# Seven block products in place of eight for the first product of an MLP, with sums of weight blocks formed by accumulating DMAs

## The chip, the cores and the metric

The kernel runs on one NeuronCore of a Trainium2 chip. The metric is device time in microseconds (us). Engines are called by the profile's names: PE is TensorE's matmul stream and PEld its weight loads, DVE is VectorE, ACT ScalarE, POOL GpSimd, SP SyncE.

## The reference

Two decoder layers on 512 tokens of 1024 channels, in fp32. Each layer runs a mixer (the first: gated MLP and latent attention; the second: gated linear attention) with an output projection, and then an MLP of inner width 4096:

```python
def sqrelu_mlp(x, w1, w2):
    return jnp.square(jax.nn.relu(x @ w1)) @ w2
...
        x = layer_norm(ALPHA * x + y, ln1_g[layer], ln1_b[layer])
        x = layer_norm(ALPHA * x + sqrelu_mlp(x, w_ff1[layer], w_ff2[layer]), ln2_g[layer], ln2_b[layer])
```

## The kernel before

**Products.** Every fp32 operand is held as a pair, hi (rounded to fp32r) and lo (the rest). A product is three matmuls, hi x hi, hi x lo and lo x hi, added up in one PSUM bank (`mm3`, L158 to L161). A weight granule of 128x1024 (512 KB, `granule`, L129) is loaded on SP's queue, cast by ScalarE to hi (L137) and reduced by VectorE to lo (L138). `to_xT` (L188) transposes a token block of the residual XN by TensorE into PSUM and splits it into XH and XL (`split`, ScalarE L164 and VectorE L165). XH and XL hold x transposed, 8 blocks of 128 channels by 512 tokens.

**The MLP.** `ff` (L276) works in four parts of the inner width. The first product of a block of 128 inner channels (`ff1_block`, L291) is 24 matmuls of 512 columns (tokens); `relu2` (L281) makes the squared relu and its pair hh, hl. The second product (`ff2_half`, L308) takes 8 inner blocks for each token block and half of the model's columns, 24 matmuls of 512 columns, and VectorE adds the result to XN (`add_cols`, L208).

**The opening.** The output projection's steps come from the generator `norms` (L243): the LayerNorm of token block t is under the products of block t+1, and its transposes stand after six of eight channel blocks of that block's second half. The norm of the last block has no products of its own behind it, so `open_blocks` (L334) computes the first four inner blocks on the first 256 tokens, 24 matmuls of 256 columns each; after three of them it transposes block 3.

**The closing.** The last part's second product is issued block by block: in the first layer through `norms` again (`close_blocks`, L362), in the second with the final norm and the stores (`close_final`, L350, `ln_store`, L225).

**What sets the order.** TensorE and VectorE run in the order in which the program writes their instructions (`manual_schedule`; for VectorE through `in_order`, L266, around the MLPs). Each engine is a queue: an instruction that waits holds all behind it. The other engines' order is the framework's. PSUM has eight banks of 128x512: six in a cycle for products, two for transposes (`BANKS`, L122).

Of the kernel before, what the change touches and what calls it, by code (L numbers as in the profile page):

```python
# [12 lines left out]
F32 = mybir.dt.float32  # L13
F32R = mybir.dt.float32r
# [89 lines left out]
def trunk(ctx: ExitStack, tc: tile.TileContext, a: dict, out: bass.AP):  # L104
# [24 lines left out]
    def granule(src, kb, cols, pool=wp, raw=None):  # L129
        """hi, lo of kb blocks of P rows by cols columns of a weight matrix."""  # L130
# [11 lines left out]
    def weave(a, b, n):  # L142
        """n pieces of a after each piece of b, until both are done."""
# [23 lines left out]
    def rsqrt_(var, n, eps=LN_EPS):  # L167
        """1/sqrt(var + eps) for a [P, n] fp32 tile, by Newton's iteration."""
# [19 lines left out]
    def to_xT(src, k0, nk, t):  # L188
        """XH/XL[:, k0:k0+nk, block t] <- the transposes of nk [P, P] blocks of src."""
# [15 lines left out]
    def add_cols(t, cols, acc, first, stats=()):  # L205
        """XN[:, t, cols] <- XN (alpha * XN at first) + acc; stats: where its statistics go, part by part."""
# [9 lines left out]
    def ln_block(t, stats):  # L216
        """XN[:, t] <- LN(XN[:, t])."""
# [7 lines left out]
    def ln_store(t, stats):  # L225
        """out[block t] <- LN(XN[:, t]); the root is ScalarE's, corrected by a step of Newton's iteration."""
# [16 lines left out]
    def norms(mm, stats):  # L243
        """The products mm(t, n, k0, k1) of half n of token block t, each block's norm under the next block's products.

        A generator: yields after each half."""
        for t in range(NT):
# [3 lines left out]
            if t > 0:  # L251
                block_T(t - 1)
# [7 lines left out]
    def act_stat(acc, lh, ll, g, per, ks, last):  # L260
        """acc += (lh + ll)[:, k, :]^T w over the blocks ks; g are granules of per blocks."""
# [11 lines left out]
    def ff1_granules(layer, f, pool=wp):  # L273
        return granules(a["w_ff1"][layer], 0, D, 4, slice(f * P, (f + 2) * P), pool)

    def ff(layer, hp, fp, xp, out_proj, prefetch):  # L276
        """The layer's MLP, after the rest of out_proj's steps; returns what prefetch returned."""
        w2 = a["w_ff2"][layer]
        hs, gr = {}, {}

        def relu2(f, acc, cols):  # L281
            hh, hl = hs[f]
            n = cols.stop - cols.start
            r = fp.tile([P, S], F32, tag="r", name="r")
            q = fp.tile([P, S], F32, tag="q", name="q")
            nc.scalar.activation(r[:, :n], acc[:, :n], AF.Relu)  # L286
            nc.scalar.activation(hh[:, cols], r[:, :n], AF.Square)  # L287
            nc.vector.tensor_tensor(q[:, :n], r[:, :n], r[:, :n], ALU.mult)  # L288
            nc.vector.tensor_tensor(hl[:, cols], q[:, :n], hh[:, cols].bitcast(F32), ALU.subtract)  # L289

        def ff1_block(f, cols=slice(0, S)):  # L291
            if f not in hs:
                hs[f] = (hp.tile([P, S], F32R, tag="hh", name="hh"), hp.tile([P, S], F32R, tag="hl", name="hl"))
            g = gr[f // 2 * 2]
            acc = bank("f1")
            n = cols.stop - cols.start
            jc = slice(f % 2 * P, (f % 2 + 1) * P)
            for k in range(KD):
                wh, wl = g[k // 4]
# [824 lines left out]
```

## Time and profile before

| what | value |
|---|---|
| median of 3 runs (lowest to highest) | 1193.89 us (1192.4 to 1194.69) |
| span of the profiled execution | 1190.5 us |
| profiled execution's own time | not given apart from its span; the runs lie 1.9 to 4.2 us above it |
| PE busy | 1174.2 us, 5880 matmul instructions |
| DVE busy | 669.3 us |
| ACT busy | 420.2 us |
| POOL busy | 4.6 us |
| moved by DMA | 111.53 MB |

The span is the time from the first to the last instruction that the profiler recorded. Busy times are sums over the instructions of an engine. The matmuls' own durations overlap, since they are pipelined; the price of one is therefore read from the distance of two starts.

### The profile page before, as it was taken

The numbers are of one execution on the slowest core, as the hardware profiler recorded it, in microseconds if no ns is written. First come the engines' busy times: TensorE is split into PE (matmuls) and PEld (weight loads), VectorE is DVE, ScalarE is ACT, GpSimd is POOL, SyncE is SP. The second block draws the span as 40 slices with busy tenths as digits, with TensorE's granted clock in tenths as the row PEclk, the third lists the DMA queues.
The fourth block names the chain that finished last, engine by engine and source line by source line (L and its number), as shares of the span: only waits on it lengthen the run. The fifth ranks groups of instructions, "written<-read, shape, count | busy, mean of one in ns | idle before, by whom it ended". The sixth has DMA issues, their size and how long they took to land.

```text
span 1190.5 us, 14854 instructions
## 1 busy us (share of the span) xinstructions
PE 1174.2 (99%) x5880; PEld 968.9 (81%) x5880; DVE 669.3 (56%) x1392; ACT 420.2 (35%) x663; POOL 4.6 (0%) x13
## 2 busy tenths in 40 slices
PE   8999999999999999999999999999999999999997
PEld 8988788988888888888888888778888888888886
DVE  6745698745245244267758569998451451451546
ACT  5466452342142133152264333332331241241410
POOL 0000000000000000000000000000000000000000
PEclk9999999999999999999999999999999999999999
DMA  8413142224134134152225312212251251251411
GB/s 251 135 36 124 44 136 63 75 93 141 36 106 141 36 107 141 36 189 72 57 92 142 106 37 71 71 53 72 75 172 36 73 174 37 72 166 46 141 36 54
DMA packets 84197, 111.53 MB, mean 94 GB/s; under 512 B 6080, under 2 KB 53056, under 8 KB 84128
## 3 DMA queue, kind: packets, MB, share of 16 engines
q1 hardware_dynamic: 84128, 110.59, 29.6%
q8 instruction: 46, 0.75, 0.3%
q14 instruction: 23, 0.19, 0.0%
HBM read 108.47 MB, written 2.10 MB: 93 GB/s over the span
## 4 chain that ended last, share of the span: by engine, by line
PE 95%; DVE 2%; ACT 1%; DMA 0%; issue 0%; SPq 0%; DVEq 0%; ACTq 0%
PE f L159 20%; PE f L161 20%; PE f L160 20%; PE vg L159 3%; PE vg L160 3%; PE vg L161 3%; PE op L159 2%; PE op L161 2%; PE op L160 2%; PE sc L607 1%; PE xt L194 1%; PE qk L159 1%; PE qk L160 1%; PE qk L161 1%; PE o L629 1%; PE pl L888 1%
## 5 line engine op out<-in xcount | busy, mean ns | idle before, releaser
L137 ACT CAST whi<-raw 128x1024 fp32r<-128x1024 f32 (+3 forms) x189 | 194.0, 1029 | 344.3 <-DMA raw<-in_w_ff 177.2
L138 DVE TENSOR_TENSOR wlo<-raw,whi 128x1024 fp32r<-128x1024 f32 (+3 forms) x189 | 220.8, 1196 | 55.7 <-ACT whi L137 55.3
L161 PE MATMUL f<-XH,wlo 128*128 128x512 f32 (+1 forms) x576 | 213.4, 370 | 0.0
L159 PE MATMUL f<-XH,whi 128*128 128x512 f32 (+1 forms) x576 | 213.3, 370 | 0.0
L160 PE MATMUL f<-XL,whi 128*128 128x512 f32 (+1 forms) x576 | 213.3, 370 | 0.0
L159 PE MATMUL f<-whi,hh 128*128 128x512 f32 (+1 forms) x520 | 203.5, 391 | 0.0
L160 PE MATMUL f<-wlo,hh 128*128 128x512 f32 (+1 forms) x520 | 203.3, 391 | 0.0
L161 PE MATMUL f<-whi,hl 128*128 128x512 f32 (+1 forms) x520 | 203.3, 391 | 0.0
L208 DVE SCALAR_TENSOR_TENSOR XN<-XN,f 128x512 f32<-128x512 f32 (+1 forms) x65 | 44.1, 678 | 191.3 <-PE f L161 191.3
L159 PEld LDWEIGHTS f<-XH,whi 128*128 128x128 f32 x576 | 108.4, 188 | 20.5
L160 PEld LDWEIGHTS f<-XL,whi 128*128 128x128 f32 x576 | 108.2, 188 | 20.3
L161 PEld LDWEIGHTS f<-XH,wlo 128*128 128x128 f32 x576 | 108.2, 188 | 20.3
L288 DVE TENSOR_TENSOR q<-r 128x512 f32<-128x512 f32 (+1 forms) x72 | 45.4, 631 | 140.0 <-ACT r L286 140.0
L160 PEld LDWEIGHTS f<-wlo,hh 128*128 128x128 f32 x520 | 97.7, 188 | 22.6
L161 PEld LDWEIGHTS f<-whi,hl 128*128 128x128 f32 x520 | 97.7, 188 | 22.6
L159 PEld LDWEIGHTS f<-whi,hh 128*128 128x128 f32 x520 | 97.7, 188 | 22.6
L286 ACT ACTIVATE r<-f 128x512 f32<-128x512 f32 (+1 forms) x72 | 39.5, 548 | 143.8 <-PE f L161 143.8
L164 ACT CAST XH<-xt 128x512 fp32r<-128x512 f32 x44 | 24.2, 588 | 91.0 <-PE xt L194 90.7
L159 PE MATMUL vg<-whi,XH 128*128 128x512 f32 x128 | 53.0, 414 | 0.0
L159 PE MATMUL op<-whi,XH 128*128 128x512 f32 x128 | 52.1, 407 | 0.2 <-ACT XH L164 0.2
L289 DVE TENSOR_TENSOR hl<-q,hh 128x512 fp32r<-128x512 f32 (+1 forms) x72 | 45.6, 633 | 9.5 <-ACT hh L287 2.6
L161 PE MATMUL op<-whi,XL 128*128 128x512 f32 x128 | 50.7, 396 | 0.0
(222 smaller groups left out, 1540.9 us busy)
## 6 DMA issues: line engine op xcount, KB each, us to landing
raw<-in_w_ff SPq DMA_DIRECT2D x128, 512.0 KB, 4.2
raw<-in_w_in_odd SPq DMA_DIRECT2D x24, 512.0 KB, 4.0
XN<-in_x SPq DMA_DIRECT2D x16, 256.0 KB, 2.9
raw<-in_w_in_even SPq DMA_DIRECT2D x8, 512.0 KB, 3.9
raw<-in_w_out_even SPq DMA_DIRECT2D x8, 512.0 KB, 3.7
raw<-in_w_out_odd SPq DMA_DIRECT2D x8, 512.0 KB, 3.4
LB<-in_ln_b SPq DMA_DIRECT2D x4, 512.0 KB, 3.8
LG<-in_ln_g SPq DMA_DIRECT2D x4, 512.0 KB, 3.8
```

Source lines behind the costliest of these rows:

```text
L137: nc.scalar.copy(hi[:, :n], raw[:, :n])
L138: nc.vector.tensor_tensor(lo[:, :n], raw[:, :n], hi[:, :n].bitcast(F32), ALU.subtract)
L159: nc.tensor.matmul(acc, lh, rh, start=first, stop=False)
L160: nc.tensor.matmul(acc, lh, rl, start=False, stop=False)
L161: nc.tensor.matmul(acc, ll, rh, start=False, stop=last)
L164: nc.scalar.copy(hi, src)
L194: nc.tensor.transpose(pt[:, j * P:(j + 1) * P], src[:, (k + j) * P:(k + j + 1) * P], ident)
L208: nc.vector.scalar_tensor_tensor(x, x, ALPHA if first else 1.0, acc, ALU.mult, ALU.add)
L286: nc.scalar.activation(r[:, :n], acc[:, :n], AF.Relu)
L288: nc.vector.tensor_tensor(q[:, :n], r[:, :n], r[:, :n], ALU.mult)
L289: nc.vector.tensor_tensor(hl[:, cols], q[:, :n], hh[:, cols].bitcast(F32), ALU.subtract)
L607: nc.tensor.matmul(sc[:, :N], qts[t][:B_QK, h, :], KT[:, h, :N], start=True, stop=True)
```

## The change

Strassen's scheme, in Winograd's form, splits the first product x W1 into 2x2 blocks: the tokens into two halves of 256, the 1024 channels into two of 512, and the inner width into two of 2048. Seven products of blocks take the place of eight. Four of them need a sum of blocks of x (s1 to s4), four a sum of blocks of the weights (t1 to t4), and the results are put together from them:

- P1 = A11 B11, P2 = A12 B21, p3 = s4 B22, p4 = A22 t4, p5 = s1 t1, p6 = s2 t2, p7 = s3 t3 (A blocks of x, B blocks of the weights).
- The work goes in 8 groups of 256 columns of each half of the inner width. `product` issues one of the seven for a group: 24 matmuls of 256 columns into the two halves of a bank. P1 and P2 add up in one bank (C11). V is p6 with P1, X is V with p5; C22, C12 and C21 are differences of X or V and the banks of p7, p3 and p4. p4 goes into the bank that p7 had. V and X lie in LG and LB, the LayerNorm's tiles; its gains are loaded after the last group.
- `terms1` makes the weights' sums. A block's raw fp32 granule is split into hi and lo, and then, in place, two accumulating DMAs of GpSimd's queue (256 KB each) add the next block of weights from HBM to it; when both have landed, the sum is split in its turn. B11 becomes t1, t2 and t4 in this way, one after the other, and B22 becomes t3. B21 is only loaded.
- `x_T` replaces `block_T` in the output projection's steps: for blocks 0 and 1 it also copies the transposes, and for blocks 2 and 3 it forms the sums of the blocks two apart: four operations and five splits on VectorE.
- The second product takes 4 inner blocks at a time (12 matmuls of 512 columns), group by group, and the closing does so with the last group.
- `wseq` is the order of the splits, `slots` that of the products; `upto` issues splits ahead of a slot, up to `TERMS`, and loads up to `LOADS` further ahead.

```diff
+    HALF_S, HK_, GF = S // 2, KD // 2, 2 * P
+    PRODUCTS = {"P1": ("A11", "B11"), "P2": ("A12", "B21"), "p3": ("s4", "B22"), "p4": ("A22", "t4"),
+                "p5": ("s1", "t1"), "p6": ("s2", "t2"), "p7": ("s3", "t3")}
+    ff_T = {}
...
-                mm3(acc[:, :n], wh[:, k % 4, jc], wl[:, k % 4, jc], XH[:, k, cols], XL[:, k, cols], k == 0, k == KD - 1)
-            relu2(f, acc, cols)
...
-        def ff2_half(p, n):
-            for t in range(NT):
-                acc = bank("f2")
-                ff2_mm(p, t, acc, gr[p, n], 0, 8)
-                add_half(t, n, acc, p == 0, None)
...
-            for f in range(4):
-                ff1_block(f, slice(0, 256))
-                if f == 2:
-                    block_T(NT - 1)
-                    items[1][0]()
-            for f in range(4):
-                ff1_block(f, slice(256, 512))
...
+        def x_T(t):
+            v = lambda z: z.rearrange("p (k c) -> p k c", k=HK_)
+            pts = []
+            for h in range(2):
+                pt = bank("xt", "tp")
+                for j in range(HK_):
+                    nc.tensor.transpose(pt[:, tb(j)], XN[:, t, (h * HK_ + j) * P:(h * HK_ + j + 1) * P], ident)
+                pts.append(pt)
+            if t < 2:
+                for h, pt in enumerate(pts):
+                    xr[t, h] = fp.tile([P, S], F32, tag="q", name="xr")
+                    nc.scalar.copy(xr[t, h], pt)
+                    operand(("A11", "A12")[h], t, v(pt))
+                return
+            s1, s2 = (fp.tile([P, S], F32, tag="q", name="sx") for _ in range(2))
+            s3, s4 = xr[t - 2, 0], xr[t - 2, 1]
+            nc.vector.tensor_tensor(s3, s3, pts[0], ALU.subtract)
+            nc.scalar.copy(s1, pts[1])
+            nc.vector.tensor_tensor(s1, s1, pts[0], ALU.subtract)
+            nc.vector.tensor_tensor(s2, s3, pts[1], ALU.add)
+            operand("s1", t, v(s1))
+            operand("s3", t, v(s3))
+            nc.vector.tensor_tensor(s4, s2, s4, ALU.subtract)
+            operand("s2", t, v(s2))
+            operand("s4", t, v(s4))
+            operand("A22", t, v(pts[1]))
...
+        w1v = lambda i, j, g: w1[i * 512:(i + 1) * 512, j * 2048 + g * GF:j * 2048 + (g + 1) * GF].rearrange(
+            "(k p) c -> p k c", p=P)
+        chains, got_w = {}, {}
+        SOURCE = {"B11": (0, 0), "B22": (1, 1), "B21": (1, 0)}
+        NEXT = {"B11": ("t1", (0, 1)), "t1": ("t2", (1, 1)), "t2": ("t4", (1, 0)), "B22": ("t3", (0, 1))}
+
+        def load1(g, n):
+            if n in SOURCE:
+                raw = chains[g, n] = xp.tile([P, WG], F32, tag="cr", name="cr", bufs=4)
+                nc.sync.dma_start(raw.rearrange("p (k c) -> p k c", k=HK_), w1v(*SOURCE[n], g))
...
+                split(hi, lo, raw)
...
+            got_w[g, n] = his, los
+            if n in NEXT:
+                to, src = NEXT[n]
+                for k in range(0, HK_, 2):
+                    nc.gpsimd.dma_start(raw.rearrange("p (k c) -> p k c", k=HK_)[:, k:k + 2], w1v(*src, g)[:, k:k + 2],
+                                        accum_op=ALU.add)
+                chains[g, to] = raw
...
+        def product(g, n):
+
+            first = (g, RELEASED[n]) not in banks
+            if first:
+                banks[g, RELEASED[n]] = bank("f1")
+            acc = banks[g, RELEASED[n]]
+            op, w = PRODUCTS[n]
+            xh, xl = ops[op]
+            his, los = got_w.pop((g, w))
+            for j in range(2):
+                d = acc[:, j * HALF_S:(j + 1) * HALF_S]
+                for k in range(HK_):
+                    for i, (l, r) in enumerate(((his[j][:, k], xh[:, k]), (his[j][:, k], xl[:, k]), (los[j][:, k], xh[:, k]))):
+                        nc.tensor.matmul(d, l, r, start=first and j == k == i == 0, stop=j == 1 and k == HK_ - 1 and i == 2,
+                                         skip_group_check=True)
...
+            V = LG[:, g % 2 * 512:(g % 2 + 1) * 512]
+            X = LB[:, g % 2 * 512:(g % 2 + 1) * 512]
...
+            def c22():
+                r = fp.tile([P, S], F32, tag="q", name="c22")
+                nc.vector.tensor_tensor(r, X, bk("d"), ALU.subtract)
+                relu2(g, 1, 1, r, r)
...
+            def c21():
+                nc.vector.tensor_tensor(bk("d"), bk("d"), V, ALU.subtract)
+                relu2(g, 1, 0, bk("d"))
+
+            step("p1s", {"P1"}, lambda: nc.scalar.copy(V, bk("a")))
+            step("V", {"p1s", "p6"}, lambda: nc.vector.tensor_tensor(V, bk("b"), V, ALU.subtract))
+            step("X", {"V", "p5"}, lambda: nc.vector.tensor_tensor(X, V, bk("e"), ALU.subtract))
+            step("C11", {"P2"}, lambda: relu2(g, 0, 0, bk("a")))
+            step("C22", {"X", "p7"}, c22)
+            step("C12", {"X", "p3"}, c12)
+            step("C21", {"V", "C22", "p4"}, c21)
...
+        def ff2_half(c, n, t):
+            acc = bank("f2")
+            ff2_mm(c, t, n, acc, 0, 4)
+            add_half(t, n, acc, c == 0, None)
...
+        FIRST = ("P1", "P2", "p5", "p7", "p6", "p3", "p4")
+        LATER = ("P1", "p3", "p5", "p7", "p6", "P2", "p4")
+        slots = [(g, n) for n in FIRST[:2] for g in range(2)] + [(g, n) for g in range(2) for n in FIRST[2:]]
+        wseq = [(g, n) for n in ("B11", "B21") for g in range(2)]
+        wseq += [(g, n) for g in range(2) for n in ("B22", "t1", "t3", "t2", "t4")]
+        for c in range(NG):
+            slots += [("w2", c, n, t) for n in range(2) for t in range(NT)] if c < NG - 1 else []
+            wseq += [("w2", c, n, h) for n in range(2) for h in range(2)]
+            if c + 2 < NG:
+                slots += [(c + 2, n) for n in LATER]
+                wseq += [(c + 2, n) for n in ("B11", "B22", "t1", "t3", "t2", "B21", "t4")]
+        place = {w: i for i, w in enumerate(wseq)}
+        at = {"load": 0, "terms": 0}
+        LOADS, TERMS = 6, 6
...
+        todo = 0
+        for _ in out_proj:
+            todo += 1
+            upto(min(todo, 4), 2)
+        for i, s in enumerate(slots):
+            if s[0] == "w2":
+                need = max(place["w2", s[1], s[2], 1], place["w2", s[1], s[2], 0])
+                upto(min(need + 1 + TERMS, need + 1 + 2 * (s[3] + 1)))
+                ff2_half(s[1], s[2], s[3])
+                continue
+            upto(place[s[0], PRODUCTS[s[1]][1]] + 1 + (TERMS if i > 3 else i))
+            product(*s)
+            if i == 0:
+                x_T(NT - 1)
+        upto(len(wseq))
+        load_ln(a["ln2_g"][layer], a["ln2_b"][layer])
+        got = prefetch() if prefetch else None
+        c = NG - 1
...
-        return norms(mm, stats)
+        return norms(mm, stats, lambda t: ff_T["now"](t))
```

**VectorE at the end of the output projection.** The place is between block 3's first half and its norm. L208 adds a half of the projection to XN, L211 and L220 make statistics, L165 are splits of the transposes of block 2. Before:

```order
L208 SCALAR_TENSOR_TENSOR XN<-XN,op 128x512 [waits PE_49]
L211 BN_STATS st<-XN 128x6 [waits DVE_49]
L165 TENSOR_TENSOR XL<-xt,XH 128x4x128 [waits Activation_49] x2
L208 SCALAR_TENSOR_TENSOR XN<-XN,op 128x512 [waits DMAHW0_49,PE_49]
L211 BN_STATS st<-XN 128x6 [waits DVE_49]
L220 BN_AGGR mv<-st 128x2 [waits DVE_49]
```

and with the change (L319 to L325 are the sums of x blocks, sl and sh their pairs):

```order
L319 TENSOR_TENSOR xr<-xr,xt 128x512 [waits PE_49]
L321 TENSOR_TENSOR sx<-sx,xt 128x512 [waits Activation_49]
L322 TENSOR_TENSOR sx<-xr,xt 128x512 [waits DVE_49,PE_49]
L165 TENSOR_TENSOR XL<-sx,XH 128x4x128 [waits Activation_49]
L165 TENSOR_TENSOR sl<-xr,sh 128x4x128
L325 TENSOR_TENSOR xr<-sx,xr 128x512 [waits DVE_49]
L165 TENSOR_TENSOR sl<-sx,sh 128x4x128 [waits Activation_49]
L165 TENSOR_TENSOR sl<-xr,sh 128x4x128 [waits Activation_49]
L165 TENSOR_TENSOR XL<-xt,XH 128x4x128
L208 SCALAR_TENSOR_TENSOR XN<-XN,op 128x512 [waits PE_49]
L211 BN_STATS st<-XN 128x6 [waits DVE_49]
L220 BN_AGGR mv<-st 128x2 [waits DVE_49]
```

Nine operations for block 2 take the place of two splits, ahead of the last half's addition and the norm of block 3.

**VectorE in the opening of the MLP.** cr is the raw granule of the first product's weights, wlo the lo part; a wait for DMASW is one for accumulating DMAs, one for DMAHW for a plain load. Before, the squared relu's operations and splits of plain granules alternate here:

```order
L289 TENSOR_TENSOR hl<-q,hh 128x256 [waits DVE_49,Activation_49]
L165 TENSOR_TENSOR XL<-xt,XH 128x4x128 [waits Activation_49] x2
L138 TENSOR_TENSOR wlo<-raw,whi 128x1024 [waits DMAHW6_49]
L138 TENSOR_TENSOR wlo<-raw,whi 128x1024 [waits DMAHW7_49]
L288 TENSOR_TENSOR q<-r 128x256 [waits Activation_49]
```

and with the change, from the split of t2 of group 0 (its split of t4 is next; then B22, t1 and t3, t2 and t4 of group 1) to V (L435), X (L436) and the difference for C22 (L423) of group 0:

```order
L165 TENSOR_TENSOR wlo<-cr,whi 128x1024 [waits DMASW7_49,DMASW6_49,Activation_49]
L165 TENSOR_TENSOR wlo<-cr,whi 128x1024 [waits DMASW1_49,DMASW0_49,Activation_49]
L165 TENSOR_TENSOR wlo<-cr,whi 128x1024 [waits DMAHW2_49,Activation_49]
L165 TENSOR_TENSOR wlo<-cr,whi 128x1024 [waits DMASW3_49,DMASW2_49,Activation_49] x2
L165 TENSOR_TENSOR wlo<-cr,whi 128x1024 [waits DMASW4_49,DMASW5_49,PE_49,Activation_49]
L165 TENSOR_TENSOR wlo<-cr,whi 128x1024 [waits DMASW6_49,DMASW7_49,PE_49,Activation_49]
L435 TENSOR_TENSOR LG<-f_2758,LG 128x512 [waits PE_49]
L436 TENSOR_TENSOR LB<-LG,f_2694 128x512 [waits DVE_49]
L423 TENSOR_TENSOR c_2785<-LB,f_2727 128x512 [waits DVE_49]
```

The three operations that put group 0's products together stand behind the splits of group 1's t2 and t4.

**TensorE and GpSimd in the same opening.** TensorE goes from p3 of group 0 (sh, sl hold s4) to p4, into the bank that the difference L423 reads:

```order
L407 MATMUL f_2793<-sl,whi 128x256
L407 MATMUL f_2793<-sh,wlo 128x256
L407 MATMUL f_2727<-XH,whi 128x256 [waits DVE_49,Activation_49]
L407 MATMUL f_2727<-XL,whi 128x256
L407 MATMUL f_2727<-XH,wlo 128x256
```

and GpSimd's queue (two DMAs a sum; the pairs shown make t3 and t2 of group 0 and, two pairs later, one sum of group 1):

```order
L359 DMA cr<-in_w_ff 128x2x256 [waits DMAHW1_49,DMAHW7_49,DVE_49,Activation_49]
L359 DMA cr<-in_w_ff 128x2x256
L359 DMA cr<-in_w_ff 128x2x256 [waits DMASW0_49,DVE_49,Activation_49]
L359 DMA cr<-in_w_ff 128x2x256 [waits DMASW1_49]
L359 DMA cr<-in_w_ff 128x2x256 [waits DMAHW0_49,DMAHW2_49,DMASW2_49,DVE_49]
L359 DMA cr<-in_w_ff 128x2x256 [waits DMASW3_49]
```

p4's first matmul waits for VectorE, and each pair of DMAs for the split that used its granule.

## Rows read from the trace of the kernel before

**Rows 1.** The page, parts 1 and 4: busy time per engine; shares of the chain.
```profile
PE 1174.2 (99%) x5880; PEld 968.9 (81%) x5880; DVE 669.3 (56%) x1392; ACT 420.2 (35%) x663; POOL 4.6 (0%) x13
...
PE 95%; DVE 2%; ACT 1%; DMA 0%; issue 0%; SPq 0%; DVEq 0%; ACTq 0%
```

**Rows 2.** Table by stage: the middle of both MLPs (stretch, length, busy, PEclk, DMA).
```profile
232.00:547.00 315.00, 315.00 (x1411) 256.43 (x1410) 134.07 (x158) 101.25 (x130) 0.00 (x0) 1.00 0.33 104
...
832.00:1140.00 308.00, 308.00 (x1383) 250.77 (x1382) 129.60 (x154) 98.13 (x128) 0.00 (x0) 1.00 0.31 98
```

**Rows 3.** Timeline of TensorE, opening of the first MLP: start us, us, instruction.
```profile
222.51 0.28 PE L159 MATMUL f<-XH,whi 128*128 128x256 f32 x1
...
231.03 0.28 PE L161 MATMUL f<-XH,wlo 128*128 128x256 f32 x1
231.15 1.04 PE L194 MATMUL xt<-ident,XN 128*128 128x128 f32 x8
231.94 0.36 PE L159 MATMUL f<-XH,whi 128*128 128x256 f32 x1
...
246.42 0.39 PE L159 MATMUL f<-XH,whi 128*128 128x512 f32 x1
...
251.55 0.40 PE L160 MATMUL f<-XL,whi 128*128 128x512 f32 x1
```

**Rows 4.** VectorE's groups by line and shape: busy us, mean ns, idle before.
```profile
L138 DVE TENSOR_TENSOR wlo<-raw,whi 128x1024 fp32r<-128x1024 f32 x178 | 211.7, 1219 | 54.6 <-ACT whi L137 54.3
...
L288 DVE TENSOR_TENSOR q<-r 128x512 f32<-128x512 f32 x56 | 38.7, 690 | 123.7 <-ACT r L286 123.7
```

**Rows 5.** ScalarE's groups by line and shape, same columns.
```profile
L137 ACT CAST whi<-raw 128x1024 fp32r<-128x1024 f32 x178 | 186.0, 1048 | 341.2 <-DMA raw<-in_w_ff 177.2 <-PE f L161 111.2 <-DMA raw<-in_w_in_odd 20.5
```

**Rows 6.** Timeline of VectorE, end of the first layer's output projection.
```profile
221.49 1.29 DVE L165 TENSOR_TENSOR XL<-xt,XH 128x512 fp32r<-128x512 f32 x2 [3.47 <-ACT XH L164]
222.71 0.69 DVE L208 SCALAR_TENSOR_TENSOR XN<-XN,op 128x512 f32<-128x512 f32 x1
...
227.50 1.29 DVE L223 SCALAR_TENSOR_TENSOR XN<-XN,ny,LB 128x1024 f32<-128x1024 f32 x1
```

**Rows 7.** The page, part 3: DMA queues and kinds (packets, MB, share).
```profile
q1 hardware_dynamic: 84128, 110.59, 29.6%
q8 instruction: 46, 0.75, 0.3%
```

**Rows 8.** DMA issues: queue, count, KB each, median us to landing.
```profile
raw<-in_w_ff SPq DMA_DIRECT2D x128, 512.0 KB, 4.2
...
XN<-in_x SPq DMA_DIRECT2D x16, 256.0 KB, 2.9
...
LB<-in_c_causal SPq DMA_DIRECT2D x1, 256.0 KB, 6.4
```

**Rows 9.** The weight granules' tile, 250 to 300 us, 512 KB loads.
```profile
DMA to landing us min/median/max: 3.3/4.4/6.1
```

**Rows 10.** Table of the last stretches; the column before DMA's is PEclk.
```profile
1182.00:1184.00 2.00, 0.54 (x5) 0.33 (x3) 1.32 (x5) 0.15 (x1) 0.00 (x0) 1.00 0.00 0
...
1186.00:1188.00 2.00, 0.00 (x0) 0.00 (x0) 1.29 (x2) 0.00 (x0) 0.00 (x0) 0.58 0.26 95
1188.00:1190.50 2.50, 0.00 (x0) 0.00 (x0) 0.00 (x0) 0.00 (x0) 0.00 (x0) 0.50 0.35 134
```

**Rows 11.** Timeline of VectorE, closing of the first layer, block 0.
```profile
548.85 0.69 DVE L208 SCALAR_TENSOR_TENSOR XN<-XN,f 128x512 f32<-128x512 f32 x1 [0.39 <-PE f L161]
...
553.63 1.28 DVE L223 SCALAR_TENSOR_TENSOR XN<-XN,ny,LB 128x1024 f32<-128x1024 f32 x1
...
559.60 1.29 DVE L165 TENSOR_TENSOR XL<-xt,XH 128x512 fp32r<-128x512 f32 x2 [3.36 <-ACT XH L164]
```

**Rows 12.** Timeline of VectorE, closing of the second layer, block 0.
```profile
1149.15 0.69 DVE L208 SCALAR_TENSOR_TENSOR XN<-XN,f 128x512 f32<-128x512 f32 x1 [3.99 <-PE f L161]
...
1153.05 1.41 DVE L240 SCALAR_TENSOR_TENSOR XN<-XN,ls,LB 128x512 f32<-128x512 f32 x2
```

More of the change, by code (lines that the diff above doesn't have):

```diff
@@ L251, in norms @@
             if t > 0:
[L252 removed]
+                (bt or block_T)(t - 1)
             mm(t, 1, 6, KD)
@@ new lines, in ff, with operand @@
+        xr = {}
+        def operand(n, t, src):
+            h, l = (z[:, :, (t % 2) * P:(t % 2 + 1) * P] for z in ops[n])
+            split(h, l, src)
+        def x_T(t):
[24 more added lines that the diff above has]
+            operand("A22", t, v(pts[1]))
@@ new lines, in terms1 @@
+        def terms1(g, n, early):
+            raw = chains.pop((g, n))
+            if early:
+                his = [hp.tile([P, HK_, P], F32R, tag="hh", name="wh") for _ in range(2)]
+                los = [hp.tile([P, HK_, P], F32R, tag="hl", name="wl") for _ in range(2)]
+                for j in range(2):
+                    split(his[j], los[j], raw.rearrange("p (k c) -> p k c", k=HK_)[:, :, tb(j)])
+            else:
+                hi, lo = wp.tile([P, WG], F32R, tag="whi", name="whi"), wp.tile([P, WG], F32R, tag="wlo", name="wlo")
+                split(hi, lo, raw)
+                his, los = ([z.rearrange("p (k c) -> p k c", k=HK_)[:, :, tb(j)] for j in range(2)] for z in (hi, lo))
+            got_w[g, n] = his, los
[5 more added lines that the diff above has]
+                chains[g, to] = raw
@@ new lines, in ff, with relu2 @@
+        hq = {}
+        def relu2(g, i, j, src, into=None):
+            hh = hp.tile([P, 2, HALF_S], F32R, tag="hh", name="hh")
+            hl = hp.tile([P, 2, HALF_S], F32R, tag="hl", name="hl")
+            r = into if into is not None else fp.tile([P, S], F32, tag="q", name="r")
+            f = lambda z: z.rearrange("p j t -> p (j t)")
+            nc.scalar.activation(r, src, AF.Relu)
+            nc.scalar.activation(f(hh), r, AF.Square)
+            nc.vector.tensor_tensor(r, r, r, ALU.mult)
+            nc.vector.tensor_tensor(f(hl), r, f(hh).bitcast(F32), ALU.subtract)
+            hq[g][i, j] = hh, hl
@@ new lines, in ff, with upto @@
+        place = {w: i for i, w in enumerate(wseq)}
+        at = {"load": 0, "terms": 0}
+        LOADS, TERMS = 6, 6
+        def upto(n, loads=None):
+            while at["load"] < min(len(wseq), n + (LOADS if loads is None else loads)):
+                w = wseq[at["load"]]
+                at["load"] += 1
+                (load2(*w[1:]) if w[0] == "w2" else load1(*w))
+            while at["terms"] < min(len(wseq), n):
+                w = wseq[at["terms"]]
+                i = at["terms"]
+                at["terms"] += 1
+                (terms2(*w[1:]) if w[0] == "w2" else terms1(*w, i < 4))
@@ L353, in close_final @@
                 st = sm.tile([P, 4, 6], F32, tag="st", name="st", bufs=8)
[L354 to L359 removed]
+                for cols in (slice(0, 512), slice(512, 768), slice(768, D)) if last else (slice(0, 512), slice(512, D)):
+                    m = cols.stop - cols.start
+                    acc = bank("f2")[:, :m]
+                    i, tc_ = t // 2, slice(t % 2 * P, (t % 2 + 1) * P)
+                    n, o = cols.start // 512, cols.start % 512
+                    for k in range(4):
+                        hh, hl = hq[c][i, k // 2]
+                        wh, wl = got_w["w2", c, n, k // 2]
+                        mm3(acc, hh[:, k % 2, tc_], hl[:, k % 2, tc_], wh[:, k % 2, o:o + m], wl[:, k % 2, o:o + m], k == 0, k == 3)
+                    add_cols(t, cols, acc, False, [st[:, i] for i in range(cols.start // 256, cols.stop // 256)])
                 ln_store(t, st)
@@ L373, in close_blocks @@
                 pass
[L375 to L397 removed]
+        (close_final if layer == DEPTH - 1 else close_blocks)()
         return got
```

130 lines of the change are left out of this document (48 added, 82 removed).

## The prediction

> **What bounds the kernel now.** The page's first and fourth parts come first [rows 1]: TensorE is busy 99% of the span, and 95% of the chain that ended last is its own work. So each microsecond in which TensorE stands still, and each microsecond of its work, is a microsecond of the kernel. The table by stage comes second [rows 2]: through the middle of either MLP TensorE is busy without a gap (315 us of 315, 308 of 308), VectorE for 134 and 130 us, ScalarE for 101 and 98. The reader is to see two things: fewer matmul columns would be gained in full, and VectorE and ScalarE have room as long as nothing makes TensorE wait for them.
>
> TensorE's timeline gives the prices [rows 3]. From 222.51 to 231.03 the 256-column matmuls start 71 steps apart, 0.120 us each; from 246.42 to 251.55 the 512-column ones 22 steps apart, 0.233 us each. Two halves cost 3% more than one whole. Each of these matmuls loads its own weights, so narrow matmuls are not held up by weight loads. Eight transposes cost 0.79 us (231.15 to 231.94).
>
> The profiled span is 1190.5 us; the profiled execution's own time is not given apart, and the three runs lie 1.9 to 4.2 us above the span, their median 3.4 above. I make the sum against the span and add 3.4. A measurement of this kernel can tell about 0.2% (2.4 us) from no change.
>
> **What is saved.** The first product of a layer takes 28 whole blocks of 24 matmuls at 0.233 us and 4 blocks in two halves, 48 matmuls at 0.120: 156.8 + 23.0 = 179.8 us. After it: 8 groups of 7 products of 24 matmuls at 0.120 = 161.3 us. That is -18.5 us a layer, **-37.0 us** in all. The second product keeps its 768 matmuls of 512 columns a layer, in groups of half the depth.
>
> **What is added beside TensorE.** From the third group on, one cycle is seven products (20.2 us) and eight halves of the second product (8 x 12 x 0.233 = 22.4): 42.6 us of TensorE. VectorE has in it 11 splits at 1.22, five combinations of products and eight operations of the squared relu at about 0.69, and eight additions at 0.69 [rows 4]: 28 us. ScalarE has 11 casts at 1.05 [rows 5], a copy and eight relu operations near 0.6: 17 us. Both fit below 42.6, so I cost this work at nothing; its cover is gone only where VectorE stands still for landings (the first rival). The loads on SyncE's queue are 512 KB each as before and six ahead of their use, so I cost them at nothing too. The second LayerNorm's loads now come after the last group's products, but 22.4 us of second products cover their landing.
>
> **Wait A: the last token block.** T is the end of the output projection's matmuls (222.51). Before, VectorE has two splits of block 2's transposes, from 221.49, then block 3's addition and norm, from 222.71 to 228.79: 6.08 us [rows 6]. TensorE covers that with 72 matmuls of 256 columns (8.64 us). Now nine operations for block 2 (four sums, five splits) stand at that place in VectorE's order. They can start about 0.6 earlier, without the cast ahead, and take 9 x 0.69 = 6.2 us: from T-1.6 to T+4.65. The norm of block 3 then ends at T+10.7. In TensorE's order only P1 of group 0 (2.88 us) stands ahead of block 3's transposes: it **waits 7.9 us**. Transposes end at T+11.6, then P1 of group 1, P2 of both: T+20.2.
>
> **Wait B: the chain of accumulating DMAs.** VectorE keeps its order. Behind block 3's nine operations (to T+17.5) come the split of B22 and C11's two operations of group 0 and the split of t1, to T+21.4. Call L the time from the end of a split to the landing of both accumulating DMAs issued on it. t2 of group 0 is cast (1.05) and split (1.22) at T+21.4+L+2.3; t4, L+2.3 later; then B22 and t1 of group 1 (1.2 each); t2 and t4 of group 1, each L+2.3 more; and only behind these stand V, X and the difference for C22 (3 x 0.72) of group 0. The first matmul of p4 of group 0 waits for that difference, since p4 goes into the bank that it reads. So p4 starts at T+21.4+4L+13.75. TensorE's work up to there is eight products and the transposes: 23.8 us. Waits A and B together cost **11.4 + 4L** a layer. The same order stands in the second layer.
>
> L is in no row: before, all data moves on one hardware queue, nothing on a software queue and nothing that accumulates [rows 7]. The nearest rows are plain loads [rows 8, 9]: 256 KB land in 2.9 us (a median), 512 KB in 3.3 at the least and 4.2 in the middle, the slowest 256 KB in 6.4. Two accumulating DMAs of 256 KB, issued one behind the other by one engine, each reading what it adds to, should lie between 3.3 us (as fast as the fastest plain load of both) and 12.8 (twice the slowest 256 KB, in series). I take 5.8, twice the 2.9, nearest to two such transfers in series. That gives 34.6 us a layer.
>
> The Trainium skill, "DMA: Bandwidth & Descriptors", section "Anatomy of one DMA — SWDGE (gpsimd) path", fits a DMA on this path by 2.0 us and the bytes over 436 KB a microsecond; no run here shows it. By that an estimate for 512 KB is 3.2 us, and the sum would come to about 1222.
>
> **The clock.** The granted clock is 1.00 up to 1184 and beyond; TensorE stops at 1182.5, and the clock reads 0.58 from 1186 and 0.50 from 1188 [rows 10]. So a long stand brings it to the lower level (1.2 of 2.4 GHz). Waits A and B hold stands of 8 us and, before p4, 23 us. What a restart costs the trace doesn't show: between nothing and half of a low stretch as long as the one seen, 2.1 us. I take 1.5 for each of two stands a layer: 3.0.
>
> Per layer the opening loses 34.6 + 3.0 = 37.6, **+75.2 us** in all.
>
> **The two closings.** The last group of the second product is half as deep: 5.6 us of TensorE a token block instead of 11.2. In the first layer VectorE needs for each block 6.1 (addition to norm), 1.4 for the other half's addition and statistics and 1.3 for the splits [rows 11]: 8.8 us, which 11.2 + 0.8 covered and 5.6 + 0.8 doesn't. TensorE waits before blocks 0, 1 and 2 are transposed 1.4, 2.2 and 2.9 us: +6.5. In the second layer VectorE's block is 1.4 + 5.25 [rows 12] against 5.6, and 1.1 us a block pile up to the end: +4. Together **+10.5**.
>
> **Sum.** 1190.5 - 37.0 + 75.2 + 10.5 = 1239.2; with 3.4 the time is **1243 us**, 4.1% slower. It moves 8 us with each microsecond of L.
>
> **The rivals.** *VectorE's order as the bound of every group.* From the difference for C22 of one group to that of the next, VectorE's order holds five operations of the squared relu and C12 with ScalarE's part between them (about 6 us), the split of B11 (1.2), three landings with a cast and a split behind each (3 x 2.27), four splits of the second product (4.9) and three combinations (2.1): 21 + 3L. That fits into the 42.6 us cycle up to L = 7.2. Beyond it every microsecond of L costs 3 us in six groups of two layers, 36 us, besides the 8: 1254 at 7.2, 1302 at 8.3, 1320 at 8.7. For it: each landing also needs GpSimd to come to its turn, and accumulating may cost a read and a write. Against it: the rows of plain loads lie below. The Trainium skill, "SBUF — State Buffer", section "Who interferes with whom", says that a VectorE operation with two inputs in SBUF contends with GpSimd's reads, and infers that writing descriptors is not held by it; no row here shows either, and a landing that waited for one split (1.22 us) would bring an estimate of 1252. Chance of L over 7.2: 0.22.
>
> *A short L.* At 3.3 the sum is 1223, at 2.5 it is 1216. Slower all the same: the break-even of the sum is at L below zero. Chance of less than 3.3: 0.05.
>
> *Faster: VectorE doesn't hold p4 behind group 1's splits.* If p4 of group 0 waits only for t4 of its own group, it starts at T+26+2L, and the loss is 2.2 + 2L a layer: at L = 3.3, 17.6 in all, one restart a layer 3.0, closings 10.5 against -37.0, which is 1188. It decides below L = 4.6 or so; at 5.8 it gives 1198. Against it: the order on VectorE is fixed by the program, and there group 1's splits stand ahead. Chance 0.10, with what else I misjudge in the same direction.
>
> *The saving isn't there*, because narrow matmuls run slower than counted: the 0.120 us is measured at full clock, weight loads included; it would leave 1280, inside the range. Chance 0.02.
>
> **How the numbers follow.** The sum with L between 3.3 and 7.2 has 0.61 (1223 to 1254), long L 0.22, short L 0.05, the case of p4 released early 0.10 and the missing saving 0.02. The range goes down to 1216 (L = 2.5) and up to 1320 (L = 8.7); it leaves out the 0.10 and about a third of the long L, 0.17. Of the 0.10 some 0.02 ends within 0.2%, and 0.01 of a still shorter L: faster by over 0.2% 0.08, within 0.03, slower 0.89.
>
> **What would show it.** In the changed profile: TensorE's stand of about 8 us before block 3's transposes, and one of about 23 us before p4 of group 0, with the granted clock at the lower level in them; four landings in series on VectorE between t1 of group 0 and V; the middle groups without gaps; a landing of the accumulating DMAs near 5.8 us. If p4 starts without a stand, or the middle has gaps in each group, the step on VectorE's order or the price of L is wrong.

## The result, and the profile after

The changed kernel takes 1551.04 us (1549.85 to 1553.25, 4 runs) against 1194.02 before: a ratio of 1.300, 95% interval 1.298 to 1.302. I had forecast 1243 and a range to 1320. The direction was right, the size was not: the loss is seven times the forecast one.

The page of the changed kernel, parts 1, 3 and 6 (columns as in [rows 1], [rows 7] and [rows 8]):

```profile
PE 1220.1 (79%) x6828; PEld 1060.3 (68%) x6828; DVE 829.1 (54%) x1604; ACT 480.6 (31%) x743; POOL 161.1 (10%) x141
...
q1 hardware_dynamic: 75680, 102.20, 21.1%
q0 software_dynamic: 34816, 33.56, 15.2%
...
cr<-in_w_ff POOLq DMA_DIRECT2D x128, 256.0 KB, 4.5
```

TensorE is busy 79% instead of 99% [rows 1]. There is a second queue, q0, with 128 DMAs of 256 KB. The median of 4.5 us from issue to landing looks harmless beside the 5.8 us that I had taken for a pair.

The table by stage (opening of the first MLP, the middle of the first, the middle of the second; columns as in [rows 2]):

```profile
222.50:315.00 92.50, 30.75 (x202) 29.20 (x200) 32.33 (x48) 19.56 (x27) 14.61 (x12) 0.66 0.31 54
...
332.00:703.00 371.00, 283.13 (x1584) 252.19 (x1584) 154.73 (x189) 93.53 (x117) 57.21 (x47) 0.87 0.41 88
...
1113.00:1487.00 374.00, 285.67 (x1584) 254.24 (x1584) 154.90 (x190) 93.90 (x118) 57.21 (x47) 0.87 0.41 87
```

The middles, without a gap before [rows 2], now leave TensorE idle for a quarter of the time, at a mean granted clock of 0.87. No other engine is full either: VectorE is busy for 155 us of 371, ScalarE for 94.

TensorE's waits (who released it; us in all, times, longest):

```profile
PE f L407 <- DVE c L423: 133.5, 16, 42.2
PE f L407 <- ACT LG L434: 98.5, 12, 10.0
...
PE xt L309 <- DVE XN L223: 15.5, 2, 7.8
```

The third line is wait A: 7.76 and 7.74 us, forecast 7.9. The first is the wait for C22's difference, 42 us in each opening where I had 23. It occurs 16 times, so in every group, where I had two. The second is in no step of the prediction: 12 times, once in every middle group, P2 waits for ScalarE's copy of P1 (L434), since it adds into the bank that the copy reads. On ScalarE that copy stands behind casts, and the first of these waits for a landing (the group whose C22 difference starts at 454.31):

```profile
442.46 1.04 ACT L164 CAST whi<-cr 128x1024 fp32r<-128x1024 f32 x1 [12.03 <-DMA cr<-in_w_ff]
443.41 1.99 ACT L164 CAST whi<-raw 128x1024 fp32r<-128x1024 f32 x2
445.30 0.58 ACT L434 COPY LG<-f 128x512 f32<-128x512 f32 x1
```

### The profile page after: what moved, and what is told of

Its sections match the earlier page's. It is cut to its first block, busy times and chain, and to the rows that moved or that the text cites. A ratio compares the mean times of both kernels' runs of the same rounds, so it can differ in the third digit from the quotient of the medians.

```text
span 1548.5 us, 17378 instructions
## 1 busy us (share of the span) xinstructions
PE 1220.1 (79%) x6828; PEld 1060.3 (68%) x6828; DVE 829.1 (54%) x1604; ACT 480.6 (31%) x743; POOL 161.1 (10%) x141
## 5 line engine op out<-in xcount | busy, mean ns | idle before, releaser
L407 PE MATMUL f<-XH,whi 128*128 128x256 f32 x448 | 157.9, 352 | 257.1 <-DVE c L423 133.5
L165 DVE TENSOR_TENSOR wlo<-cr,whi 128x1024 fp32r<-128x1024 f32 x104 | 125.7, 1222 | 365.1 <-ACT whi L164 365.1
L164 ACT CAST whi<-cr 128x1024 fp32r<-128x1024 f32 x104 | 106.1, 1045 | 532.4 <-DMA cr<-in_w_ff 529.1
L359 POOL DMA_DIRECT2D cr<-in_w_ff x128 | 155.9, 1218 | 1013.9 <-issue 478.0
L407 PE MATMUL f<-XH,wlo 128*128 128x256 f32 x448 | 151.1, 337 | 1.8 <-DVE wlo L165 1.8
L407 PE MATMUL f<-XL,whi 128*128 128x256 f32 x448 | 151.6, 338 | 0.0
L407 PE MATMUL f<-sh,whi 128*128 128x256 f32 x384 | 111.7, 291 | 19.4 <-ACT whi L164 19.4
L407 PE MATMUL f<-sh,wlo 128*128 128x256 f32 x384 | 111.2, 290 | 1.9 <-DVE wlo L165 1.9
L407 PE MATMUL f<-sl,whi 128*128 128x256 f32 x384 | 110.7, 288 | 0.0
L165 DVE TENSOR_TENSOR wlo<-raw,whi 128x1024 fp32r<-128x1024 f32 x64 | 75.6, 1220 | 42.4 <-ACT whi L164 42.4
L208 DVE SCALAR_TENSOR_TENSOR XN<-XN,f 128x512 f32<-128x512 f32 x129 | 81.8, 676 | 12.9 <-PE f L161 12.8
```

What stands on the lines that cost most here:

```text
L164: nc.scalar.copy(hi, src)
L165: nc.vector.tensor_tensor(lo, src, hi.bitcast(F32), ALU.subtract)
L208: nc.vector.scalar_tensor_tensor(x, x, ALPHA if first else 1.0, acc, ALU.mult, ALU.add)
L359: nc.gpsimd.dma_start(raw.rearrange("p (k c) -> p k c", k=HK_)[:, k:k + 2], w1v(*src, g)[:, k:k + 2], accum_op=ALU.add)
L407: nc.tensor.matmul(d, l, r, start=first and j == k == i == 0, stop=j == 1 and k == HK_ - 1 and i == 2, skip_group_check=True)
```

## The account of 358 us

The spans differ by 1548.5 - 1190.5 = 358.0 us. TensorE's timeline of the changed kernel gives the borders, in the opening of the first MLP:

```profile
233.19 1.94 PE L309 MATMUL xt<-ident,XN 128*128 128x128 f32 x8 [7.76 <-DVE XN L223]
...
314.88 0.55 PE L407 MATMUL f<-XH,whi 128*128 128x256 f32 x1 [42.18 <-DVE c L423]
...
331.99 0.38 PE L407 MATMUL f<-XH,whi 128*128 128x256 f32 x1 [0.48 <-DVE c L423]
```

The last two lines are the first matmuls of p4 of groups 0 and 1. The first P1 matmul is at 222.40, so p4 of group 1 starts 109.6 us later. Its thirteen products and the transposes ahead are 38.2 us of work: 71.4 us lost, and 70.2 in the second layer (1004.88 to 1113.24). From there six groups take 371.5 us to p4 of group 7 (703.51), and 374.3 in the second layer, at 42.6 each instead of 61.9: 116 and 119 lost. The saving stands at 37.0. What is left, 358.0 + 37.0 - 141.6 - 235.0 = 18.4 us, lies in the closings and the rest. The measured losses in the table are counted against 38.2 us for an opening and 42.6 for a middle group.

| step | forecast, us | measured, us |
|---|---|---|
| fewer columns | -37.0 | -37.0 (taken as forecast) |
| two openings, clock included | +75.2 | +141.6 |
| twelve middle groups | 0 | +235.0 |
| closings and the rest | +10.5 | +18.4 |

The timeline of GpSimd in the first opening (start us, us; in brackets the idle time ahead):

```profile
243.49 1.21 POOL L359 DMA_DIRECT2D cr<-in_w_ff  x1 [33.63 <-ACT hh L386]
248.36 1.22 POOL L359 DMA_DIRECT2D cr<-in_w_ff  x1 [3.66 <-issue]
253.12 1.21 POOL L359 DMA_DIRECT2D cr<-in_w_ff  x1 [3.53 <-issue]
258.55 1.22 POOL L359 DMA_DIRECT2D cr<-in_w_ff  x1 [4.22 <-DMA cr<-in_w_ff]
266.09 1.21 POOL L359 DMA_DIRECT2D cr<-in_w_ff  x1 [6.32 <-DVE wlo L165]
270.76 1.22 POOL L359 DMA_DIRECT2D cr<-in_w_ff  x1 [3.46 <-issue]
```

VectorE's timeline, the splits of t1 and t2 (two rows):

```profile
244.85 1.22 DVE L165 TENSOR_TENSOR wlo<-cr,whi 128x1024 fp32r<-128x1024 f32 x1
...
264.45 1.22 DVE L165 TENSOR_TENSOR wlo<-cr,whi 128x1024 fp32r<-128x1024 f32 x1 [7.95 <-ACT whi L164]
```

and ScalarE's, the cast of the sum t2 and that of t4 (with two more of the kind):

```profile
263.38 1.04 ACT L164 CAST whi<-cr 128x1024 fp32r<-128x1024 f32 x1 [9.46 <-DMA cr<-in_w_ff]
275.53 2.94 ACT L164 CAST whi<-cr 128x1024 fp32r<-128x1024 f32 x3 [11.10 <-DMA cr<-in_w_ff]
```

The last pair makes t4 of group 0. Its split of t2 ends at 265.67, the DMAs start at 266.09 and 270.76, and ScalarE can cast at 275.53: **L is 9.9 us**. GpSimd is busy 1.2 us with a DMA, yet starts the next only 4.7 us or more after the one before, as long as that takes to land. In the whole trace none of the 128 starts while another is under way, and most start 0.3 us behind the landing of the one before. "issue" in the brackets says that the profile shows nothing that GpSimd waited for. Where t3's pair stands ahead (243.49 and 248.36), t2's, whose split of t1 ended at 246.07, starts at 253.12 and can be cast at 263.38: 17.3 us.

From the split to the cast, the four landings between t1 of group 0 and V take 17.3, 9.9, 18.1 and 9.9 us, 55.15 together. In place of 4L in the prediction's own chain that gives 55.15 + 13.75 = 68.9 us from the end of t1's split (246.07) to p4 of group 0; measured 68.8. In the second layer it is 68.0 and 68.0.

In the middle, with L = 9.9 and 9.4 for one pair ahead, the rule of the first rival gives a cycle of 21 + 3 x 9.9 + 9.4 = 60 us. Measured: 61.9. The size fits better than the parts: in the group whose difference is at 454.31 the pairs of t1, t3 and t2 run one behind another, and the four pairs take 40.6 us where the rule has 39.1, while ScalarE's copy and P2, which stand between t4's landing and the next difference, are not in the rule. There t4's first DMA took longer to land, and the second started that much later (GpSimd's timeline, then the landing of the first):

```profile
431.15 1.21 POOL L359 DMA_DIRECT2D cr<-in_w_ff  x1 [6.19 <-DVE wlo L165]
437.90 1.21 POOL L359 DMA_DIRECT2D cr<-in_w_ff  x1 [5.54 <-issue]
...
DMA to landing us min/median/max: 6.4/6.4/6.4
```

Why it took longer, no run shows.

## The experiments

Theories: **Q**, the software queue's room for descriptors lets GpSimd issue only one such DMA until it has landed; **G**, GpSimd needs 4.7 us to prepare one; **A**, adding in the DMA engines is slow; and, apart from these, that VectorE's order alone makes the loss. The runs e1 to e6 are single ones; the kernel before took 1192 us (the median) beside them.

**e1_plain.**

```diff
-                    nc.gpsimd.dma_start(raw.rearrange("p (k c) -> p k c", k=HK_)[:, k:k + 2], w1v(*src, g)[:, k:k + 2],
-                                        accum_op=ALU.add)
+                    nc.gpsimd.dma_start(raw.rearrange("p (k c) -> p k c", k=HK_)[:, k:k + 2], w1v(*src, g)[:, k:k + 2])
```

> The change with the same DMAs on GpSimd's queue, but overwriting in place of adding (so the sums of weight blocks are left out). Theory Q (the software queue has room for only one accumulating DMA of 256 rows at a time, so GpSimd holds the next back until the one before has landed: starts 4.7 us apart): a plain DMA needs less of that room, starts come about 1.2 us apart, a pair lands 6 to 7 us after its split, and the time falls to 1350 to 1450 us. Rival G (GpSimd needs 4.7 us to prepare each DMA, adding or not): no change, 1540 to 1560 us. Rival A (adding itself is slow in the DMA engines): as fast as under Q; the next run tells them apart.

Measured: 1268.35 us, below what Q gave. GpSimd's timeline shows a pair from 254.08:

```profile
254.08 1.44 POOL L359 DMA_DIRECT2D cr<-in_w_ff  x2 [5.78 <-DVE wlo L165]
```

Two DMAs, 0.72 us each, without a pause. On the page they land in 3.4 us (the median):

```profile
cr<-in_w_ff POOLq DMA_DIRECT2D x128, 256.0 KB, 3.4
```

G falls for plain DMAs. Q and A are both left.

**e2_quarter.**

```diff
-                for k in range(0, HK_, 2):
-                    nc.gpsimd.dma_start(raw.rearrange("p (k c) -> p k c", k=HK_)[:, k:k + 2], w1v(*src, g)[:, k:k + 2],
+                for k in range(HK_):
+                    nc.gpsimd.dma_start(raw.rearrange("p (k c) -> p k c", k=HK_)[:, k:k + 1], w1v(*src, g)[:, k:k + 1],
```

Each DMA now adds one block of 128 rows, 128 KB.

> The change with each sum made by four accumulating DMAs of 128 KB in place of two of 256 KB. Theory Q: three of these have room at once, starts come 1 to 2 us apart, and four land 6 to 8 us after the split in place of 9.9: 1380 to 1460 us. Rival G by the piece: four starts at 4.7 us, a landing after 19 us, over 1800 us. Rival G by the row, and rival A: the same total, 1520 to 1570 us.

Measured: 1352.8 us, better than Q had it and against G and A, which gave no gain. The same bytes are added in the same order, by twice as many DMAs, and it is 198 us faster. GpSimd's timeline:

```profile
260.15 2.67 POOL L359 DMA_DIRECT2D cr<-in_w_ff  x3 [5.84 <-DVE wlo L165]
263.51 0.87 POOL L359 DMA_DIRECT2D cr<-in_w_ff  x1 [0.69 <-issue]
```

Three start back to back (0.6 us apart), the fourth 0.3 us behind the landing of the first: room for three, and then a wait.

**e5_room.**

```diff
...
-    nc = bacc.Bacc("TRN2", target_bir_lowering=False, num_devices=1, dynamic_dma_scratch_size=1024)
+    nc = bacc.Bacc("TRN2", target_bir_lowering=False, num_devices=1, dynamic_dma_scratch_size=2048)
```

> The change with 2048 instead of 1024 bytes of each SBUF partition reserved for the software queue's descriptors, and nothing else but two small pools cut to make room (buffers of small tiles 6 to 4, of one mixer tile 3 to 2). The DMAs are those of the change: pairs of 256 KB, accumulating. Theory Q (room): the next DMA no longer waits for the landing of the one before, starts come 1.2 us apart, a pair lands about 6.5 us after its split, the cycle of a middle group falls from 62 to 45 to 52 us, and the time to 1270 to 1370 us. Rival G (GpSimd's own preparation of 4.7 us): no change, 1540 to 1560 us.

Measured: 1363.15 us, inside Q's range. The DMAs are the change's own; twice the room alone takes 188 us off. GpSimd's timeline:

```profile
257.95 2.45 POOL L359 DMA_DIRECT2D cr<-in_w_ff  x2 [7.38 <-DVE wlo L165]
268.38 3.71 POOL L359 DMA_DIRECT2D cr<-in_w_ff  x3 [7.98 <-DVE wlo L165]
```

and the DMA issues on its page (median us from issue to landing last):

```profile
cr<-in_w_ff POOLq DMA_DIRECT2D x128, 256.0 KB, 5.7
```

The pair now starts in one go, 0.7 us apart, and three in a row do; the fourth starts 0.3 us behind the landing of the first, and nowhere in the trace are more than three under way. Q is shown in this: the room decides how many of these DMAs are under way at once, and the next one starts when one has landed. That the room is filled by descriptors, no trace shows. A keeps a part: side by side these adding DMAs land in 5.7 us, the plain ones of e1_plain in 3.4, and 95 us lie between the two kernels' times.

**e3_none** and **e4_hw.**

```diff
-                for k in range(0, HK_, 2):
-                    nc.gpsimd.dma_start(raw.rearrange("p (k c) -> p k c", k=HK_)[:, k:k + 2], w1v(*src, g)[:, k:k + 2],
-                                        accum_op=ALU.add)
+                nc.sync.dma_start(raw.rearrange("p (k c) -> p k c", k=HK_), w1v(*src, g))
```

The line with + stands in e4_hw only.

> The change without the accumulating DMAs (each chain is split again from the same granule, so the sums of weight blocks are left out); everything else as in the change, with all its splits. If the whole loss hangs on the landings: my formula with L = 0 gives 1190.5 - 37.0 + 28.8 (11.4 a layer and 3 of clock) + 10.5 + 3.4 = 1196 us, with TensorE without gaps in the middle of the MLPs. Rival: the order on VectorE and ScalarE costs time by itself: 1230 us or more, with gaps in every group.

> The change with one plain 512 KB load on SyncE's queue in place of each pair of accumulating DMAs, at the same place and with the same waits (so the sums of weight blocks are left out). If only L counts: L is about 5 us (0.4 to the issue and 4.5 to land), and the formula gives 1236 us. Rival: SyncE's queue stands at each of these loads until the split before it is done, the later plain loads stand behind it, and the time is 1260 to 1350 us.

Measured: 1204.2 and 1235.95 us. TensorE's largest waits in e3_none:

```profile
PE xt L309 <- DVE XN L223: 15.6, 2, 7.8
PE f L404 <- DVE c L420: 8.7, 4, 3.3
```

and in e4_hw:

```profile
PE f L405 <- DVE c L421: 40.9, 4, 19.9
PE xt L309 <- DVE XN L223: 15.5, 2, 7.8
```

Without landings the middle cycle is 42.6 us, TensorE's own work; with e4_hw's loads the openings alone wait. L as the prediction defines it, here from a split to the next cast, is 3.7 to 5.5 us in e4_hw's openings, 4.5 in the mean of eight. From the first P1 to p4 of group 1 the two openings of e4_hw take 145.5 us, those of e3_none 107.7: 37.9 us more for 4.5 us of L, 8.4 us each; the prediction had 8. e3_none lies 8 us above the formula: its openings lose 2.5 us more than that has, its closings and the rest some 7 more. That e4_hw hits its 1236 is in part luck: the closings and the rest cost 6 us more, the middles 5 less. So the structure of the sum holds, and the rival of e3_none (the order costs by itself) falls but for 8.7 us.

The middle cycle (mean of six, from the starts of C22's difference in the first layer) by run:

| run | median landing, us | cycle, us | time, us |
|---|---|---|---|
| the change | 4.5, one at a time | 61.9 | 1551.0 |
| e5_room | 5.7, side by side | 50.5 | 1363.2 |
| e2_quarter | 3.5 for each quarter | 48.7 | 1352.8 |
| e1_plain | 3.4, not adding | 44.6 | 1268.4 |
| e4_hw | 3.9 for 512 KB, hardware queue | 42.2 | 1236.0 |
| e3_none | none | 42.6 | 1204.2 |

**e6_order.**

```diff
-            upto(place[s[0], PRODUCTS[s[1]][1]] + 1 + (TERMS if i > 3 else i))
+            upto(place[s[0], PRODUCTS[s[1]][1]] + 1 + (TERMS if i > 8 else 2 if i > 3 else i))
```

> The change with one thing moved in the opening: VectorE forms V, X and C22 of group 0 ahead of the splits of group 1's t1 to t4, not behind them. If the landings themselves are the bound there: p4 of group 0 starts some 35 us earlier, but group 1's sums still land one after the other, so only TensorE's 14 us of group 1's products move under them: 12 to 18 us less a layer, 1510 to 1530 us. Rival (the order on VectorE alone makes the loss of the opening): the stand of 42 us before p4 goes, about 1465 us.

Measured: 1540.76 us, 10 less, under my 20 to 40; only 3 of the 10 lie in the openings (0.1 and 2.7 us less up to p4 of group 1). TensorE's timeline shows p4 of group 0 early, as expected:

```profile
282.15 0.55 PE L407 MATMUL f<-XH,whi 128*128 128x256 f32 x1 [8.21 <-DVE c L423]
```

That is 33 us before the change's 314.88. C22's difference of group 1, on VectorE's timeline of the change and then of e6_order:

```profile
331.25 0.69 DVE L423 TENSOR_TENSOR c<-LB,f 128x512 f32<-128x512 f32 x1
...
331.29 0.69 DVE L423 TENSOR_TENSOR c<-LB,f 128x512 f32<-128x512 f32 x1
```

It comes no earlier in the first layer. The landings, not the order, bound the opening; this falsifies the prediction's rival of p4 released early, which priced group 0 and forgot group 1.

**best1.** The sums on VectorE, the loads on SyncE's queue:

```diff
...
+        TERM = {"t1": ("B11", "B12"), "t3": ("B12", "B22"), "t2": ("B11", "B22"), "t4": ("B11", "B21")}
+
+        def add(g, n):
+            x, y = (raws[g, z] for z in TERM[n])
+            nc.vector.tensor_tensor(x, x, y, ALU.add)
...
```

> The seven products without GpSimd: all four weight blocks of a group come by plain 512 KB loads on SyncE's queue, and VectorE adds them in place (four additions of 1.22 us a group). Block 3's transposes stand behind four products instead of one; the sums for group 0 are begun under the output projection; V, X and C22 of a group stand ahead of the next group's splits; the closing takes the last two groups together, 11.2 us a token block as before. If the products' saving of 37.0 us is real and only waits ate it: waits of 3 to 8 us a layer in the opening remain, and 1190.5 - 37.0 + 12 + 4 (clock) + 3.4 gives 1173 us (1165 to 1185). Rival: VectorE, with 33 us of work in 42.6 and more in the opening, holds TensorE in every group: above 1194 us.

Measured: 1247.16 us, ratio 1.0466 (1.0448 to 1.0483); the rival's side. TensorE's timeline shows a wait that I had built in:

```profile
232.72 0.58 PE L428 MATMUL f<-XH,wh 128*128 128x256 f32 x1 [8.08 <-ACT LG L437]
```

P2 adds into P1's bank, so it needs ScalarE's copy of P1 into V; V lay in LG, which the norm of block 3 still reads. In the middle VectorE's own order was a loop of about 44 us a group: each split stood behind its sum and waited for the cast between.

**best2.** Parts of the edit, against best1:

```diff
...
+        EARLIER = {"t1": ("t1", "t3"), "t3": ("t2",), "B21": ("t4",)}
...
-                nc.vector.tensor_tensor(r, r, r, ALU.mult)
+            nc.scalar.activation(r, r, AF.Square)
...
+        VX = [wp.tile([P, WG], F32, tag="raw", name="vx", bufs=3) for _ in range(2)]
...
```

> best1 with four repairs of what its trace shows: V and X of the first two groups lie in two granules of the loads' pool and no longer in the LayerNorm's tiles (TensorE stood 8 us until the norm of block 3 had used them); each addition of weight blocks stands one split ahead of its own split on VectorE, so that ScalarE's cast lies between; the fp32 square of the relu is ScalarE's (VectorE loses one operation of 0.69 us per block); V, X and C22 stand ahead of the second product's splits. If the remaining loss of best1 is VectorE's order and that stand: the cycle of a middle group falls from 43.9 to 42.6 us, the opening loses about 5 us a layer instead of 25, and the time is 1172 to 1195 us. Rival: VectorE is bound by its load in the opening whatever the order: 1205 to 1235 us.

Measured: 1189.16 us, ratio 0.9971 (0.9959 to 0.9984). The middle cycle is 42.3 us and the openings lose about 5 us each, so the rival falls. Four things were changed at once; what each is worth, the runs don't show. One larger wait was left at each closing:

```profile
533.97 0.80 PE L161 MATMUL f<-whi,hl 128*128 128x512 f32 x1 [6.67 <-DVE hl L412]
```

**best3.** Parts of the edit, against best2:

```diff
...
+            if s[0] == NG - 1:
+                flush()
+                upto(at_ + {"p6": 4, "P2": 5}.get(s[1], TERMS))
...
+            for k, _ in enumerate(norms(mm, stats)):
+                if k == 1 and prefetch:
+                    got.extend(prefetch())
...
```

> best2 with two changes at the closing, where its trace shows TensorE waiting 13.7 us for the lo parts of the relu that stand behind six splits on VectorE: for the last group the lo parts come ahead of the splits, and the next mixer's weights are split after block 0's norm instead of before all. If that wait and its two restarts of the clock are all that is left there: 1170 to 1177 us. Rival: the splits move into TensorE's way, and nothing is gained: 1185 to 1192 us.

Measured: **1176.26 us, ratio 0.9862 (0.9842 to 0.9882)**, faster than both kernels (the one before took 1192.56 beside it). Its page, parts 1 and 4:

```profile
PE 1145.9 (97%) x6840; PEld 997.9 (85%) x6840; DVE 845.8 (72%) x1588; ACT 517.6 (44%) x807; POOL 5.4 (0%) x13
...
PE 87%; DVE 7%; ACT 3%; DMA 1%; issue 1%; SPq 0%; DVEq 0%; ACTq 0%
```

TensorE is the chain again. The seven products are worth their columns when nobody waits for a sum: 16 of the 37 us are kept, the rest is still lost in the openings and closings.

## Why the prediction was wrong

- **What bounds the kernel, and the saving**: right. With the sums off the path, best2's middle runs at 42.3 us a group against a forecast 42.6.
- **Wait A**: right, 7.76 us against 7.9.
- **Wait B**: VectorE's chain and the slope of 8 us for each us of L were right (e3_none to e4_hw: 8.4; with the landings as measured the chain comes to 68.9 us for 68.8). Its size was off, for the next point.
- **L is the step that failed.** "I take 5.8, twice the 2.9, nearest to two such transfers in series": the two were in series, but each takes 4.7 us with its issue, so L is 9.9. And I had measured L from a split to its own landing, on a queue of its own; it is one queue for all sums, and t3's pair stands ahead of t2's, so two of the four landings in each opening take 16.6 to 18.4 us. Their mean is 13.7, beyond even my bound of 12.8. I had even put in a sentence that "each landing also needs GpSimd to come to its turn", and given it no price.
- **The first rival** was what happened, at a chance of 0.22: VectorE's order, standing still at landings, became the bound of every group, and the twelve middle groups that I had put at nothing lost 235 us. Its rule (21 + 3L) with the measured L and the pair ahead gives 60 us a cycle for 61.9, though it leaves out ScalarE, which stands still at the same landings and holds P2 (98.5 us). My range stopped at L = 8.7 although my own bounds for L reached 12.8: at 36 us and more for each us, the range had to reach as far as the bound did.
- **The Trainium skill's fit** ("DMA: Bandwidth & Descriptors", section "Anatomy of one DMA — SWDGE (gpsimd) path": 2.0 us and the bytes over 436 KB a us, an estimate of 2.6 us for 256 KB) does not agree with these traces: plain DMAs on this path landed in 3.4 us (3.0 at the least), adding ones in 4.5 alone and 5.7 side by side. The measurement decides.
- **The clock**: 1.5 us a restart was low, and there were more of them. The two stands that I priced cost 2.2 us each in the first opening: behind wait A (233.19 to 237.89) at a granted clock of 0.52, and in p4's first 23 steps (314.88 to 319.85, 4.97 us in place of 2.76) at 0.51. After the stand before p6 of group 0 TensorE starts 0.213 us apart and then 0.12:

```profile
266.11 0.41 PE L407 MATMUL f<-sh,whi 128*128 128x256 f32 x1
...
268.46 0.33 PE L407 MATMUL f<-sh,wlo 128*128 128x256 f32 x1
268.62 0.28 PE L407 MATMUL f<-sh,whi 128*128 128x256 f32 x1
268.75 0.28 PE L407 MATMUL f<-sl,whi 128*128 128x256 f32 x1
```

From 266.11 to 268.46 there are 11 steps at the slower pace, 1.0 us lost in this piece alone; the low pace begins at 264.48. There were stands in every group, not two a layer: in the two middles TensorE is busy 569 us, at a mean clock of 0.87, for work that takes 511 at full clock, so the clock's part in their 235 us is, as an estimate, 58.
- **The closings**: 18.4 us against 10.5, with the rest of the program in it. e3_none, without any landing, has some 18 there too, so this miss has another cause than L; it was not taken apart further.

## What to carry to other kernels

Price a transfer that is in a dependent chain by its queue, not by its median landing: how many can be under way at once, and what else stands in that queue. When a term has a slope of 36 us for each microsecond of an unknown, the range must go to the end of what that unknown may be. And follow a wait through every engine whose queue it enters: here ScalarE stood still at the same landings as VectorE. Small sums whose result is needed soon were cheaper here on an engine with room (four additions of 1.22 us a group on VectorE) than as DMAs; best2 also set each one place ahead of the split that needs it.

## What the runs showed of the hardware

- With a room of 1024 bytes (`dynamic_dma_scratch_size`), an adding DMA of 256 rows was alone under way: the next started 4.7 us or more after it, mostly 0.3 us behind its landing. With 2048 bytes three were under way, started 0.7 us apart. In 1024 bytes three adding DMAs of 128 rows had room, or three plain ones of 256 rows.
- An adding DMA of 256 KB kept GpSimd busy for 1.21 us alone and landed in 4.5 us, in 5.7 with others beside it; a plain one took 0.72 and 3.4 us.
- GpSimd's time for such a DMA was 1.21 to 1.22 us throughout the opening, with VectorE's operations beside it (at 243.49 the square and the difference of a relu) or without (at 248.36). The Trainium skill ("SBUF — State Buffer", section "Who interferes with whom") infers that the writing of descriptors is not held by VectorE's operations with two inputs; these rows agree.
